# A float32r decoder block on one core: two products traded in each up pair, the down weights' low half by VectorE, and weight preparation in three steps

## The chip, the core and the metric

One core of one Trainium2 chip runs the whole program. The metric is device time in microseconds for one execution. A profiled execution also has a span, from its first instruction to its last, which is a little shorter than its time.

## The reference

One decoder block over 512 positions and 16 prepended meta tokens (528 in all), width 1024, in float32. The first half (attention, pooling, gates) is not touched. The second half is a gated MLP with a short convolution:

```python
h = h + (gate_a * y_a + gate_b * y_b) @ w_o[l]
hn = rmsnorm(h, norm2_g[l])
up = causal_dwconv(hn @ w_up[l], conv_w[l], conv_b[l])
a, bv = jnp.split(up, 2, axis=-1)
h = h + (jax.nn.silu(a) * bv) @ w_down[l]
...
return rmsnorm(h, final_norm_g)[:, N_META:]
```

`w_up` is 1024 x 5632 and `w_down` 2816 x 1024.

## The kernel before

Activations lie with channels on the 128 partitions and positions along the row. To keep float32 accuracy with float32r matmuls, each operand is split in a high half (the value rounded to float32r) and a low half (the value less its high half), and each product is three matmuls: high by high, high by low, low by high.

The MLP is a list `seq` of 38 jobs (lines 630 to 637). 22 are up jobs; job `up i` computes block `i` of `a` and block `i` of `bv` together, called an up pair here. 16 are down jobs, each two 128-row output blocks of `w_down` over one of four parts of the gated rows: parts 0 to 2 have six blocks of 128 rows (36 matmuls of 512 columns a job), part 3 has four (24). Two down jobs stand behind each of up 9, 10, 15 and 16; the other eight stand at the end, the last four of them (part 3) in a loop of their own (lines 856 to 889), where the final norm is worked in.

Up jobs 0 to 3 (`up_plain`, line 720) are plain products, while the four operand sets for the rest are made (`cross`, line 752). Up jobs 4 to 21 (`up_fast`, line 780) replace eight block products by seven, Strassen's way, each 4 x 3 = 12 matmuls of 258 columns into a PSUM bank (`seven`, line 771). Three products use weight blocks directly (`g`), four use sums of weight blocks (`sa`, `sb`). They run in this order: `x`, `q`, `v`, `x`, `y`, `x`, `q`. The second and third `x` add onto the first in the same bank, and the second `q` onto the first; between them ScalarE copies the running value out: `z11` (line 788), `z22` (790), `z12` (793), `z21` (797). So PE may not start the third `x` product before `z12` has been copied.

Four things make a job's weights:
- `fetch` (line 640): SP loads the raw tile, 1 MB for an up pair, 768 or 512 KB for a down job. There are three raw buffers (`raw`).
- `make_own` with `high_and_low` (lines 653 to 677): ScalarE writes the rounded negative of the raw weights to the low tile (`gl`, line 654), POOL issues DMAs that add the raw weights from memory onto it (line 656: three pieces of 256 KB for an up pair, two for a down job), and ScalarE copies the raw weights to the high tile (`gh`, line 657). There are two buffers of each, so those of job n + 2 are free when PE has ended job n.
- `make_sums` (line 682), for up jobs only: VectorE adds raw blocks in place (line 692, four adds), and `split` (line 248: a ScalarE copy at 249, a VectorE subtraction at 250) makes high and low halves of `sa` and `sb`.
- `prepare(n)` at the end of job n fetches for jobs n + 2 and n + 3 and calls `make_own(n + 2)`; in a fast up job those instructions are queued behind the `z21` copy. `weights(n)` at the start of job n calls `make_sums` for n and n + 1.

Each engine runs its queue in order. The framework (Tile) sets that order when the program is built: an instruction that it reckons to be ready sooner may be put ahead of one that the program lists earlier, and `tc.issue_after(ins)` forces what is traced in it, on the engine of `ins`, behind `ins`. It also makes the waits.

After up job i comes `conv(i - 3)` (line 808): the convolution taps, the gate and the split of the gated rows, on ScalarE and VectorE. After the last up job come the convolutions that are left.

Of the kernel before, what the change touches and what calls it, by code (L numbers as in the profile page):

```python
# [9 lines left out]
F32R = mybir.dt.float32r  # L10
BF16 = mybir.dt.bfloat16
I32 = mybir.dt.int32
AF = mybir.ActivationFunctionType
ALU = mybir.AluOpType

P = 128
# [20 lines left out]
PLAIN = 4  # L37
LAG = 3
CROSS = {(0, 1): 0, (1, 0): 1, (1, 1): 2, (2, 0): 3}
PARTS = ((0, 6), (6, 6), (12, 6), (18, 4))  # L40
# [28 lines left out]
def hybrid_block(ctx: ExitStack, tc: tile.TileContext, xt, g1d, wts, wup, wdown, wglr, wgk, vecs, out):  # L69
# [178 lines left out]
    def split(hi, lo, src):  # L248
        act.activation(hi, src, AF.Copy)
        dve.tensor_tensor(lo, src, f32(hi), ALU.subtract)  # L250
# [47 lines left out]
    for k in range(KT):  # L298
        for m in range(2):
            hi, lo = preps[m]  # L300
# [266 lines left out]
    for m in range(8):  # L567
        hi, lo = chunk(ORDER["grp"] + m // 4)
        acc = ps(f"pgrp{m}")
        g = m // 2  # L570
# [69 lines left out]
    def fetch(n):  # L640
        if n >= len(seq) or n in loaded:
            return
        job = seq[n]
        t = rawp.tile([P, 4, 512], F32, tag="raw", name=f"raw{n}")
        if job[0] == "up":
            sp.dma_start(t, wup[job[1]])
        else:
            nk = PARTS[job[1]][1]
            flat_t = t.rearrange("p a b -> p (a b)")
            sp.dma_start(flat_t[:, 0 : 2 * nk * P], wdown[4 * job[1] + job[2], :, 0 : 2 * nk * P])  # L650
        loaded[n] = t

    def high_and_low(hi, lo, src, dram, pieces):
        act.activation(lo, src, AF.Copy, scale=-1.0)  # L654
        for piece in pieces:
            pool.dma_start(lo[piece], dram[piece], accum_op=ALU.add)  # L656
        act.activation(hi, src, AF.Copy)  # L657

    def blocks(t):
        return t.rearrange("p a (k n) -> p a k n", n=P)  # L660

    def make_own(n):
        if n >= len(seq) or n in own:
            return
        fetch(n)
        job, raw = seq[n], loaded[n]
        hl = [gp.tile([P, 3, 512], F32R, tag=f"g{c}", name=f"g{c}{n}") for c in "hl"]
        if job[0] == "down":
            k = 2 * PARTS[job[1]][1] * P
            hi, lo, src = (t.rearrange("p a b -> p (a b)")[:, 0:k] for t in (*hl, raw))  # L670
            halves_of = [(slice(None), slice(c * k // 2, (c + 1) * k // 2)) for c in range(2)]
            high_and_low(hi, lo, src, wdown[4 * job[1] + job[2], :, 0:k], halves_of)
            own[n] = [t.rearrange("p (c k n) -> p c k n", c=2, n=P) for t in (hi, lo)]
            return
        order = (2, 0, 1) if job[1] >= PLAIN else (1, 2, 0)
        high_and_low(*hl, raw[:, 0:3], wup[job[1], :, 0:3], [(slice(None), b) for b in order])
        own[n] = [blocks(t) for t in hl]

    def two(name):
        return tuple(ssp.tile([P, 2, 4, P], F32R, tag=f"s{c}", name=f"s{c}_{name}") for c in "hl")  # L680
# [1 line left out]
    def make_sums(n):  # L682
        if n >= len(seq) or n in sums or seq[n][0] == "down":
            return
        raw = loaded[n]
        if seq[n][1] < PLAIN:
            x = two(f"{n}x")
            split(*(t[:, 0:1] for t in x), blocks(raw[:, 3:4]))
            sums[n] = (x,)
            return  # L690
        for dst, x in ((0, 3), (3, 2), (2, 0), (1, 2)):
            dve.tensor_tensor(raw[:, dst], raw[:, dst], raw[:, x], ALU.add)  # L692
        sums[n] = (two(f"{n}a"), two(f"{n}b"))
        split(*sums[n][0], blocks(raw[:, 0:3:2]))
        split(*sums[n][1], blocks(raw[:, 1:4:2]))

    def weights(n):
        make_sums(n)
        make_sums(n + 1)
        return (own[n], *sums.get(n, ()))  # L700

    def prepare(n, behind=None):
        fetch(n + 2)
        fetch(n + 3)
        if behind is None:
            make_own(n + 2)
        else:
            with tc.issue_after(behind.ins):
                make_own(n + 2)

    for n in range(2):
        make_own(n)

    def pairtile(name, dt=F32):
        return flat(name, unitp, dt)
# [3 lines left out]

    def up_plain(n, i):  # L720
        g, x = weights(n)
        z = pairtile(f"z{i}").rearrange("p (a b) -> p a b", a=2)
        for c in range(2):
            accs = [bank(f"pup{i}_{c}{h}") for h in range(2)]
            for k in range(KT):
                w = [
                    (x[e][:, 0, k // 2] if k % 2 else g[e][:, 0, k // 2]) if c
                    else g[e][:, 2 if k % 2 else 1, k // 2]
                    for e in range(2)
                ]  # L730
                for e, (p, q) in enumerate(((0, h2h), (0, h2l), (1, h2h))):
                    for acc, (a, b) in zip(accs, TAIL):
                        pe.matmul(  # L733
                            acc[:, 0 : b - a], w[p], q[k][:, a:b],
                            start=k == 0 and e == 0, stop=k == KT - 1 and e == 2,
                        )
            if i == 0 and c == 0:
                s2 = [bank(f"n2s{h}") for h in range(2)]
                for q, first_q in ((sh, True), (sl, False)):
                    for acc, (a, b) in zip(s2, TAIL):  # L740
                        pe.matmul(acc[:, 0 : b - a], ones, q[:, a:b], start=first_q, stop=not first_q)
                rsqrt_mean(rstd2, s2, TAIL, D, n2t)
            for src, cols in parts_of(accs, TAIL):
                dve.tensor_tensor(z[:, c, cols], src, rstd2[:, cols], ALU.mult)
            if (i, c) in CROSS:
                cross(CROSS[i, c])
        prepare(n)
        zs[i] = z
# [22 lines left out]
    def seven(acc, w, block, x, at, first=True):  # L771
        for k in range(4):
            for e, (a, b) in enumerate(((0, 0), (0, 1), (1, 0))):
                pe.matmul(  # L774
                    acc[:, 0:HN], w[a][:, block, k], x[k][b][:, at],
                    start=first and k == 0 and e == 0, stop=k == 3 and e == 2,
                    skip_group_check=not first,
                )

    def up_fast(n, i):  # L780
        g, sa, sb = weights(n)
        z = pairtile(f"z{i}").rearrange("p (a b) -> p a b", a=2)
        z11, z12 = (z[:, 0, a:b] for a, b in HALF)
        z21, z22 = (z[:, 1, a:b] for a, b in HALF)
        x, y, q, v_ = (bank(f"{c}{i}") for c in "xyqv")
        n_ = slice(0, HN)
        seven(x, g, 2, direct, 2)
        act.activation(z11, x[:, n_], AF.Copy)
        seven(q, sa, 0, crossed, 1)
        act.activation(z22, q[:, n_], AF.Copy)  # L790
        seven(v_, g, 0, crossed, 3)
        seven(x, sa, 1, crossed, 2, False)
        act.activation(z12, x[:, n_], AF.Copy)
        seven(y, g, 1, direct, 0)
        dve.tensor_tensor(z11, y[:, n_], z11, ALU.add)
        seven(x, sb, 1, crossed, 0, False)
        behind = act.activation(z21, x[:, n_], AF.Copy, scale=-1.0)
        dve.tensor_tensor(z22, z21, z22, ALU.subtract)
        dve.tensor_tensor(z21, v_[:, n_], z21, ALU.add)
        seven(q, sb, 0, direct, 1, False)  # L800
        dve.tensor_tensor(z12, q[:, n_], z12, ALU.add)
        prepare(n, behind)
        zs[i] = z

    gated = {}
# [28 lines left out]
    for n, job in enumerate(seq):  # L834
        if job[0] == "up":
            i = job[1]
            (up_plain if i < PLAIN else up_fast)(n, i)
            if i >= LAG:
                conv(i - LAG)
            if i == FF - 1:  # L840
                for k in range(FF - LAG, FF):
                    conv(k)
                table(LOG_EXP, silus[-1])
        elif job[1] < 3:
            (w,) = weights(n)
            for c in range(2):
                acc = bank(f"pd{n}_{c}")
                down(acc, w, c, job[1], (0, 512))
                h = h2[2 * job[2] + c][:, META:]
                dve.tensor_tensor(h, acc, h, ALU.add)  # L850
            prepare(n)
# [3 lines left out]
    base = len(seq) - 4  # L855
    for m in range(7):
        (w,) = weights(base + m // 2)
        if m % 2:
            prepare(base + m // 2)
        acc = bank(f"pe{m}")  # L860
        down(acc, w, m % 2, 3, (0, 512))
        h = h2[m][:, META:]
        dve.tensor_tensor(h, acc, h, ALU.add)
        if m == 0:
            act.activation(tot3, h, AF.Square)
        else:
            sq = pairtile(f"n3_sq{m}")[:, 0:512]
            act.activation(sq, h, AF.Square)
            (pool if m < 5 else dve).tensor_tensor(tot3, tot3, sq, ALU.add)
        act.activation(h, h, AF.Copy, scale=v1("gf", m))  # L870
# [94 lines left out]
```

## Time and profile before

| what | value |
|---|---|
| time, median of 3 runs | 854.01 us (851.27 to 854.12) |
| the profiled execution's own time | 854.07 us |
| its span | 852.4 us |
| mean granted TensorE clock | 0.994 of full |
| VectorE, ScalarE busy from 778 to 812 us | 17.74, 18.53 us of 34 |
| raw loads of up pairs | 22 of 1024 KB, median 8.0 us to landing |

Rows of the profile give the line of the kernel, the engine, the operation, the tile written and the tiles read (buffer numbers left out), the shape and a count. PE is the matmul engine, PEld its weight load, DVE is VectorE, ACT is ScalarE, POOL is GpSimd, SP the queue that issues plain loads. "Idle before, releaser" is the time in which an engine had nothing to run, and what ended it. In rows in order of time the first number is the start and the second the duration. Matmuls overlap, so the distance of two starts, not the duration, is what one costs. The MLP begins at about 476 us.

### The profile page before, as it was taken

The page shows a single profiled execution, that of the slowest core. Times are in us where ns is not written, and L with a number is a line of the kernel's source. Part 1 is how long each engine was busy: PE and PEld are TensorE (multiplying, and loading weights), DVE is VectorE, ACT ScalarE, POOL GpSimd, SP SyncE. Part 2 cuts the span into 40 slices and gives each one's busy share as a digit, 9 for nine tenths or more (in the row PEclk, how much of TensorE's full clock was granted, in tenths as well). Part 3 has the DMA queues.
Part 4 walks back from the last instruction along what each step waited for, and adds up shares of the span by engine and source line. Part 5 has one row for each costly group of instructions (what it writes and reads, how often), then busy time and mean ns, then how long its engine had stood idle before and what let it go on. Part 6 is the DMA issues. An engine that isn't in the chain of part 4 may idle for free.

```text
span 852.4 us, 15085 instructions
## 1 busy us (share of the span) xinstructions
PE 827.7 (97%) x6357; PEld 795.8 (93%) x6357; DVE 526.2 (62%) x817; ACT 440.4 (52%) x622; POOL 144.2 (17%) x149
## 2 busy tenths in 40 slices
PE   8999999999999999999999999999999999999993
PEld 6999999999999999999999999998899987999772
DVE  6677335379756433355555488995569844897425
ACT  7287134266234212353263357885568854777562
POOL 3000000001740000000022122221222222221241
PEclk9999999999999999999999999999999999999997
DMA  7423221122323322362275074867977777877763
GB/s 240 128 64 110 76 75 50 33 77 66 118 81 99 100 86 89 100 198 83 92 248 173 1 172 100 194 154 198 216 167 161 183 177 184 185 162 174 152 92 102
DMA packets 35780, 109.96 MB, mean 129 GB/s; under 512 B 4000, under 2 KB 6816, under 8 KB 32896
## 3 DMA queue, kind: packets, MB, share of 16 engines
q1 hardware_dynamic: 20368, 79.10, 27.8%
q0 software_dynamic: 14112, 28.84, 20.5%
q8 instruction: 50, 0.82, 0.4%
q10 hardware_dynamic: 1232, 1.05, 0.4%
q14 instruction: 18, 0.15, 0.0%
HBM read 106.88 MB, written 2.10 MB: 128 GB/s over the span
## 4 chain that ended last, share of the span: by engine, by line
PE 79%; DMA 7%; ACT 6%; DVE 5%; issue 2%; SPq 0%; DVEq 0%; POOL 0%; ACTq 0%
PE pd L829 9%; PE pu L150 5%; PE pv L150 5%; PE po L150 5%; PE pb L150 5%; PE pgb L150 5%; PE pga L150 5%; PE pr L150 5%; PE pa L150 5%; PE x L774 5%; DMA gl<-in_wdown_dram 5%; PE pup L733 4%; PE q L774 4%; PE pq L150 3%; DVE raw L692 2%
## 5 line engine op out<-in xcount | busy, mean ns | idle before, releaser
L133 ACT ACTIVATE whi<-wraw 128x1024 fp32r<-128x1024 f32 (+2 forms) x78 | 78.9, 1014 | 202.5 <-PE pa L150 36.4
L134 DVE TENSOR_TENSOR wlo<-wraw,whi 128x1024 fp32r<-128x1024 f32 (+2 forms) x78 | 94.8, 1218 | 13.0 <-ACT whi L133 7.2
L656 POOL DMA_DIRECT2D gl<-in_wup_dram x66 | 59.1, 1219 | 226.7 <-ACT gl L654 215.4
L829 PE MATMUL pd<-g,gh 128*128 128x512 f32 (+1 forms) x304 | 93.2, 388 | 0.0
L657 ACT ACTIVATE gh<-raw 128x1536 fp32r<-128x1536 f32 (+1 forms) x38 | 54.5, 1435 | 47.1 <-issue 26.1
L829 PEld LDWEIGHTS pd<-g,gh 128*128 128x128 f32 x304 | 56.5, 188 | 11.9
L829 PE MATMUL pd<-g,gl 128*128 128x512 f32 (+1 forms) x152 | 59.3, 390 | 3.2 <-DMA gl<-in_wdown_dram 3.2
L692 DVE TENSOR_TENSOR raw<-raw 128x512 f32<-128x512 f32 x72 | 49.5, 688 | 15.6 <-ACT gl L654 12.0
L654 ACT ACTIVATE gl<-raw 128x1536 fp32r<-128x1536 f32 (+1 forms) x38 | 54.4, 1431 | 0.8 <-DMA raw<-in_wup_dram 0.5
L535 POOL TENSOR_TENSOR pt<-u 128x1028 f32<-128x1028 f32 (+3 forms) x4 | 14.0, 3498 | 191.9 <-ACT whi L133 179.0
L656 POOL DMA_DIRECT2D gl<-in_wdown_dram x32 | 28.1, 1040 | 106.1 <-ACT gl L654 94.7
L850 DVE TENSOR_TENSOR h<-pd,h 128x512 f32<-128x512 f32 x24 | 16.5, 689 | 42.9 <-PE pd L829 42.8
L829 PEld LDWEIGHTS pd<-g,gl 128*128 128x128 f32 x152 | 28.6, 188 | 10.8 <-DMA gl<-in_wdown_dram 3.8
L815 DVE SCALAR_TENSOR_TENSOR cv<-z,vec,cv 128x512 f32<-128x512 f32 x44 | 32.7, 748 | 9.1 <-ACT cv L814 9.0
L814 ACT ACTIVATE cv<-z,vec 128x512 f32<-128x512 f32 x44 | 34.0, 812 | 0.0
L816 DVE SCALAR_TENSOR_TENSOR cv<-z,vec,cv 128x512 f32<-128x512 f32 x44 | 32.5, 747 | 0.2
L150 PE MATMUL pr<-xh,whi 128*128 128x258 f32 (+1 forms) x128 | 26.1, 285 | 0.0
L150 PE MATMUL pv<-xh,wlo 128*128 128x264 f32 x128 | 26.0, 285 | 0.0
L150 PE MATMUL pu<-xh,wlo 128*128 128x258 f32 (+3 forms) x128 | 25.9, 284 | 0.0
L150 PE MATMUL pv<-xl,whi 128*128 128x264 f32 x128 | 25.9, 284 | 0.0
L150 PE MATMUL pu<-xh,whi 128*128 128x258 f32 (+3 forms) x128 | 25.9, 284 | 0.0
L150 PE MATMUL pu<-xl,whi 128*128 128x258 f32 (+3 forms) x128 | 25.9, 284 | 0.0
(821 smaller groups left out, 2756.2 us busy)
## 6 DMA issues: line engine op xcount, KB each, us to landing
wraw<-in_wts_dram SPq DMA_DIRECT2D x72, 512.0 KB, 3.6
raw<-in_wup_dram SPq DMA_DIRECT2D x22, 1024.0 KB, 8.0
gl<-in_wup_dram POOLq DMA_DIRECT2D x66, 256.0 KB, 7.4
raw<-in_wdown_dram SPq DMA_DIRECT2D x12, 768.0 KB, 7.9
gl<-in_wdown_dram POOLq DMA_DIRECT2D x24, 384.0 KB, 8.1
h<-in_xt_dram SPq DMA_DIRECT2D x4, 514.0 KB, 6.0
raw<-in_wdown_dram SPq DMA_DIRECT2D x4, 512.0 KB, 4.8
gl<-in_wdown_dram POOLq DMA_DIRECT2D x8, 256.0 KB, 5.7
```

The lines of the kernel that those rows point to most:

```text
L133: act.activation(hi[:, a:b], t[:, a:b], AF.Copy)
L134: dve.tensor_tensor(lo[:, a:b], t[:, a:b], f32(hi[:, a:b]), ALU.subtract)
L150: pe.matmul(acc[:, s, : b - a], w, x[:, a:b], start=(i == 0 and w is wh and x is xh), stop=(i == n - 1 and last),)
L654: act.activation(lo, src, AF.Copy, scale=-1.0)
L656: pool.dma_start(lo[piece], dram[piece], accum_op=ALU.add)
L657: act.activation(hi, src, AF.Copy)
L692: dve.tensor_tensor(raw[:, dst], raw[:, dst], raw[:, x], ALU.add)
L733: pe.matmul(acc[:, 0 : b - a], w[p], q[k][:, a:b], start=k == 0 and e == 0, stop=k == KT - 1 and e == 2,)
L774: pe.matmul(acc[:, 0:HN], w[a][:, block, k], x[k][b][:, at], start=first and k == 0 and e == 0, stop=k == 3 and e == 2, skip_group_check=n ...
L814: act.activation(cv, z[:, c, META:], AF.Identity, scale=v1("cw2", m), bias=v1("cb", m))
L815: dve.scalar_tensor_tensor(cv, z[:, c, META - 1 : L - 1], v1("cw1", m), cv, ALU.mult, ALU.add)
L829: pe.matmul(acc, w[p][:, c, k], gated[k0 + k][q][:, a:b], start=k == 0 and e == 0, stop=k == nk - 1 and e == 2,)
```

## The change

In `up_fast` the order of the last two products is traded: `x`, `q`, `v`, `x`, `y`, `q`, `x`. The `z12` addition follows `q`, and `z21` is now copied from the last product.

`make_own` is split in two functions and a shared one. `direct_tiles(n)` takes the two tiles. `make_low(n)` makes the low tile of an up job as before (ScalarE negative, POOL DMAs) and does nothing for a down job. `make_high(n)` copies the high tile of an up job; for a down job it calls `split`, so that ScalarE makes the high tile and VectorE subtracts for the low one, with no DMA.

The calls move. `make_low(n + 2)` stays at the end of job n, behind the `z21` copy in fast up jobs. `make_high(n + 1)` and `make_sums(n + 1)` are called in job n: at its start in plain up jobs and down jobs, behind the `z11` copy in fast up jobs (the sums follow it in the program, without the forced order). Before the first job only `make_low(0)` and `make_low(1)` are called.

```diff
+    def make_low(n):
+        if n >= len(seq) or seq[n][0] == "down" or n in low_made:
             return
...
+        act.activation(lo, loaded[n][:, 0:3], AF.Copy, scale=-1.0)
+        for b in (2, 0, 1) if i >= PLAIN else (1, 2, 0):
+            pool.dma_start(lo[:, b], wup[i, :, b], accum_op=ALU.add)
+
+    def make_high(n):
...
+        _, (hi, lo), k = direct_tiles(n)
+        if k is None:
+            act.activation(hi, loaded[n][:, 0:3], AF.Copy)
+        else:
+            split(hi, lo, loaded[n].rearrange("p a b -> p (a b)")[:, 0:k])
...
     def weights(n):
+        make_low(n)
+        make_high(n)
         make_sums(n)
-        make_sums(n + 1)
-        return (own[n], *sums.get(n, ()))
-
-    def prepare(n, behind=None):
+        return (own[n][0], *sums.get(n, ()))
+
+    def behind(ins, made, n):
+        if ins is None:
+            return made(n)
+        with tc.issue_after(ins.ins):
+            made(n)
+
+    def prepare(n, ins=None):
         fetch(n + 2)
         fetch(n + 3)
...
+        behind(ins, make_low, n + 2)
...
         seven(x, g, 2, direct, 2)
-        act.activation(z11, x[:, n_], AF.Copy)
+        behind(act.activation(z11, x[:, n_], AF.Copy), make_high, n + 1)
+        make_sums(n + 1)
         seven(q, sa, 0, crossed, 1)
...
         dve.tensor_tensor(z11, y[:, n_], z11, ALU.add)
+        seven(q, sb, 0, direct, 1, False)
+        dve.tensor_tensor(z12, q[:, n_], z12, ALU.add)
         seven(x, sb, 1, crossed, 0, False)
-        behind = act.activation(z21, x[:, n_], AF.Copy, scale=-1.0)
+        turned = act.activation(z21, x[:, n_], AF.Copy, scale=-1.0)
         dve.tensor_tensor(z22, z21, z22, ALU.subtract)
         dve.tensor_tensor(z21, v_[:, n_], z21, ALU.add)
-        seven(q, sb, 0, direct, 1, False)
-        dve.tensor_tensor(z12, q[:, n_], z12, ALU.add)
-        prepare(n, behind)
+        prepare(n, turned)
...
         elif job[1] < 3:
             (w,) = weights(n)
+            make_high(n + 1)
+            make_sums(n + 1)
...
         (w,) = weights(base + m // 2)
+        make_high(base + m // 2 + 1)
```

More of the change, by code (lines that the diff above doesn't have):

```diff
@@ L651, in fetch @@
         loaded[n] = t
[L653 to L657, printed above, removed]
     def blocks(t):
         return t.rearrange("p a (k n) -> p a k n", n=P)
-    def make_own(n):
-        if n >= len(seq) or n in own:
-            return
[L665 to L673, printed above, removed]
-            return
-        order = (2, 0, 1) if job[1] >= PLAIN else (1, 2, 0)
-        high_and_low(*hl, raw[:, 0:3], wup[job[1], :, 0:3], [(slice(None), b) for b in order])
-        own[n] = [blocks(t) for t in hl]
@@ new lines, in hybrid_block, with direct_tiles @@
+    low_made, high_made = set(), set()
+    def direct_tiles(n):
+        if n not in own:
+            fetch(n)
+            job = seq[n]
+            hl = [gp.tile([P, 3, 512], F32R, tag=f"g{c}", name=f"g{c}{n}") for c in "hl"]
+            if job[0] == "down":
+                k = 2 * PARTS[job[1]][1] * P
+                hl = [t.rearrange("p a b -> p (a b)")[:, 0:k] for t in hl]
+                own[n] = [t.rearrange("p (c k n) -> p c k n", c=2, n=P) for t in hl], hl, k
+            else:
+                own[n] = [blocks(t) for t in hl], hl, None
+        return own[n]
@@ new lines, in make_low @@
+    def make_low(n):
+        if n >= len(seq) or seq[n][0] == "down" or n in low_made:
+            return
+        low_made.add(n)
+        _, (hi, lo), _ = direct_tiles(n)
+        i = seq[n][1]
+        act.activation(lo, loaded[n][:, 0:3], AF.Copy, scale=-1.0)
+        for b in (2, 0, 1) if i >= PLAIN else (1, 2, 0):
+            pool.dma_start(lo[:, b], wup[i, :, b], accum_op=ALU.add)
+    def make_high(n):
+        if n >= len(seq) or n in high_made:
+            return
+        high_made.add(n)
+        _, (hi, lo), k = direct_tiles(n)
+        if k is None:
+            act.activation(hi, loaded[n][:, 0:3], AF.Copy)
+        else:
+            split(hi, lo, loaded[n].rearrange("p a b -> p (a b)")[:, 0:k])
@@ L697, in weights @@
     def weights(n):
+        make_low(n)
+        make_high(n)
         make_sums(n)
-        make_sums(n + 1)
-        return (own[n], *sums.get(n, ()))
-    def prepare(n, behind=None):
+        return (own[n][0], *sums.get(n, ()))
[5 more added lines that the diff above has]
+    def prepare(n, ins=None):
         fetch(n + 2)
         fetch(n + 3)
[L705 to L712, printed above, removed]
+        behind(ins, make_low, n + 2)
+    make_low(0)
+    make_low(1)
     def pairtile(name, dt=F32):
@@ L845, in hybrid_block @@
             (w,) = weights(n)
+            make_high(n + 1)
+            make_sums(n + 1)
             for c in range(2):
```

## The prediction

> **What bounds the kernel now.** I read the page's engine table first, then the busy time by stage, the waits of PE, and last the rows of single instructions around each wait.
>
> ```profile
> PE 827.7 (97%) x6357; PEld 795.8 (93%) x6357; DVE 526.2 (62%) x817; ACT 440.4 (52%) x622; POOL 144.2 (17%) x149
> ```
>
> PE is busy nearly throughout, so its matmuls are the floor, and an edit that takes none away (this one takes none: the same seven products, the same down products) can only win back what PE idles. The edited code runs from about 476 us to the end. There PE waits for these (columns: who waited for whom, total us, times, longest):
>
> ```profile
> PE pd L829 <- DMA gl<-in_wdown_dram: 3.2, 4, 1.7
> PE x L774 <- ACT z L793: 1.2, 6, 0.2
> ```
> ```profile
> PE pe L829 <- DMA gl<-in_wdown_dram: 0.7, 2, 0.5
> PE pup L733 <- DMA gl<-in_wup_dram: 0.6, 1, 0.6
> ```
>
> The low half of a down weight arrives late six times (3.9 us), and the third `x` product of an up pair waits six times for the copy `z12` (1.2 us). VectorE looks far from full at 62%, but that is a mean over unlike stages (columns by stretch: length, then busy time and count of PE, PEld, DVE, ACT, POOL):
>
> ```profile
> 544.00:554.00 10.00, 10.00 (x86) 10.00 (x85) 10.00 (x18) 8.85 (x14) 2.64 (x3) 1.00 0.77 183
> 647.00:657.50 10.50, 10.29 (x87) 10.09 (x86) 10.11 (x17) 8.38 (x13) 2.64 (x3) 1.00 0.72 162
> ```
>
> Where up pairs follow one another, DVE has no gap in the first stretch and little in the second. VectorE work added to such a job would move the end; where it is added decides.
>
> **Part 1: the down weights' low half by VectorE.** An idle entry understates what a stall costs, because it counts from the modelled end of a matmul that others would have overlapped:
>
> ```profile
> 710.00 0.50 PE L829 MATMUL pd<-g,gl 128*128 128x512 f32 x1 [1.70 <-DMA gl<-in_wdown_dram]
> 710.33 0.61 PE L829 MATMUL pd<-g,gh 128*128 128x512 f32 x2
> 710.78 0.39 PE L829 MATMUL pd<-g,gl 128*128 128x512 f32 x1
> ```
>
> Two matmuls start in 710.78 - 710.33 = 0.45 us, 0.23 each, while one is shown as 0.39: a stall hides 0.16 more. The matmul behind the stalled one starts 0.33 later, not 0.23: 0.10 more. Six stalls therefore cost 3.9 + 6 x 0.26 = 5.5 us. Their cause is a chain as long as a job (rows of ACT, then of the chain that ended last):
>
> ```profile
> 601.74 1.49 ACT L657 ACTIVATE gh<-raw 128x1536 fp32r<-128x1536 f32 x1 [1.57 <-PE pd L829]
> 603.13 1.47 ACT L654 ACTIVATE gl<-raw 128x1536 fp32r<-128x1536 f32 x1
> ```
> ```profile
> 604.89 7.67 DMA gl<-in_wdown_dram
> 612.61 16.41 PE pd L829 x70
> ```
>
> A `g` buffer is free when the job two places earlier ends (601.7); two copies and 7.67 us of accumulating DMA later it is 612.56, and PE has been waiting. A down job lasts 16.41 / 2 = 8.2 us. The new chain has no DMA: copy `gh`, then one DVE subtraction. No row has that subtraction at 1536 columns; two rows of the same line give its slope:
>
> ```profile
> L657 ACT ACTIVATE gh<-raw 128x1536 fp32r<-128x1536 f32 x32 | 47.3, 1479 | 35.5 <-PE pd L829 16.8 <-issue 15.3 <-PE pup L733 3.4
> L250 DVE TENSOR_TENSOR g<-cv,g 128x512 fp32r<-128x512 f32 x22 | 15.2, 689 | 6.2 <-ACT g L249 6.2
> L250 DVE TENSOR_TENSOR xl<-t,xh 128x1032 fp32r<-128x1032 f32 x4 | 4.9, 1232 | 2.6 <-ACT xh L249 2.6
> L657 ACT ACTIVATE gh<-raw 128x1024 fp32r<-128x1024 f32 x4 | 4.2, 1060 | 11.6 <-issue 10.7 <-PE pe L829 0.9
> ```
>
> (1232 - 689) / 520 = 1.044 ns a column, so 1232 + 504 x 1.044 = 1758 ns for 1536 columns and about 1.22 us for 1024. The chain is 1.48 + 1.76 = 3.2 us within 8.2, and in the last four 1.06 + 1.22 = 2.3 us within twice the distance of these rows, 5.6:
>
> ```profile
> 815.29 0.69 DVE L863 TENSOR_TENSOR h<-pe,h 128x512 f32<-128x512 f32 x1 [2.09 <-PE pe L829]
> 818.07 0.69 DVE L863 TENSOR_TENSOR h<-pe,h 128x512 f32<-128x512 f32 x1 [2.08 <-PE pe L829]
> ```
>
> DVE gains 12 x 1.76 + 4 x 1.22 = 26 us of work. It lies in down jobs and in the up job ahead of a pair of them, and that up job makes no sums for its successor: it loses four adds and two splits and gains one split. So PE sees nothing of it: 0 us, and all 5.5 won. If the cover fails, the price is the rival A below. ACT loses 16 copies, POOL 32 DMA issues, the 16 DMA engines 11.3 MB; none sets the pace.
>
> **Part 2: the traded products.** Now `z12` has one product (`y`) of time before PE writes that bank again:
>
> ```profile
> 646.01 0.28 PE L774 MATMUL y<-dl,gh 128*128 128x258 f32 x1
> 646.13 0.28 PE L774 MATMUL y<-dh,gl 128*128 128x258 f32 x1
> 646.62 0.39 PE L774 MATMUL x<-xh,sh_16b 128*128 128x258 f32 x1 [0.20 <-ACT z L793]
> 646.84 0.28 PE L774 MATMUL x<-xl,sh_16b 128*128 128x258 f32 x1
> ```
>
> Here 0.49 passes in place of 0.12, then 0.22 in place of 0.12: 0.47 us, six times, 2.8 us. The copy is late because it stands behind a longer loop on ACT:
>
> ```profile
> 638.12 1.48 ACT L654 ACTIVATE gl<-raw 128x1536 fp32r<-128x1536 f32 x1
> ...
> 640.45 1.48 ACT L657 ACTIVATE gh<-raw 128x1536 fp32r<-128x1536 f32 x1
> ...
> 645.23 1.06 ACT L249 ACTIVATE sh_17a<-raw 128x1024 fp32r<-128x1024 f32 x1 [0.84 <-DVE raw L692]
> 646.20 0.36 ACT L793 ACTIVATE z<-x 128x258 f32<-128x258 f32 x1
> ```
>
> `z21` releases `gl`, then `gh`, then DVE's sums, then `sh_17a`, then `z12`, then PE, then the next `z21`. That closes each 10.5 us. With `q` between `y` and `x` the copy has 12 x 0.12 = 1.43 us more, against a lateness of 0.37: the loop opens and 2.8 us are won, if nothing else delays the copy (part 3). `q`'s own copy `z22` is four products old by then: 0.
>
> **Part 3: three separate steps.** `gh` of the next job is now queued behind `z11`, after `gl`, and the sums wait for it. The job in the rows above began five products, 7.2 us, ahead of 646.25 (where its third `x` would have begun without the stall), at 639.1. There `gh` ended at 641.9, 2.8 us in, and `z12` at 646.56, 7.5 us in. After the change ACT does `z21` (0.1 us in), `gl`, `z11` and `gh`; a wide copy takes 1.39 us there before the next starts (601.74 to 603.13), a narrow one like `z21` 0.28 (542.75 to 543.03, rows below), so `gh` ends 0.1 + 2 x (0.28 + 1.39) = 3.4 us in, 0.6 later. If `z12` stays behind `sh_a` it ends 8.1 us in, and PE wants it six products, 8.6 us in: 0.5 us to spare, 0 lost. In plain pairs and down jobs nothing orders `gh` behind `gl`; the rows at 601.74 show `gh` first although the program lists it second, so I leave the 0.6 us of the plain pair where it is (bounds: 0 to 0.85 won, at the cost per stall above).
>
> What moves for the worse is `gl` of an up pair behind `z21`, now the last product's copy, 1.43 us later. POOL's DMAs and all that waits in POOL's queue behind them move too (rows of ACT, POOL; then DMA issues: count, KB, us to landing):
>
> ```profile
> 542.75 0.39 ACT L797 ACTIVATE z<-x 128x258 f32<-128x258 f32 x1 [0.49 <-PE x L774]
> ```
> ```profile
> 544.81 2.64 POOL L656 DMA_DIRECT2D gl<-in_wup_dram  x3 [7.41 <-ACT gl L654]
> ```
> ```profile
> gl<-in_wup_dram POOLq DMA_DIRECT2D x1, 256.0 KB, 4.4
> ```
> ```profile
> raw<-in_wup_dram SPq DMA_DIRECT2D x1, 1024.0 KB, 5.9
> gl<-in_wup_dram POOLq DMA_DIRECT2D x1, 256.0 KB, 7.7
> ```
> ```profile
> gl<-in_wdown_dram POOLq DMA_DIRECT2D x1, 384.0 KB, 9.5
> ```
> ```profile
> DMA to landing us min/median/max: 3.9/7.4/13.6
> ```
>
> The first piece leaves 2.06 us behind the start of `z21`, which will be about 0.1 us into the next job: issue at +2.1. The job after needs it at 7 x 1.43 + 0.24 = +10.3. It may take 8.2 us. It took 4.4 where the 1 MB raw load came later, 7.7 where that load went out with it (the two rows are one answer, for 526.2 to 526.55). So 0.5 us is left in the worst like case: 0 us. [...]
>
> **Sum.** The profiled execution took 854.07 us (span 852.4), 0.06 over the median 854.01. 854.07 - 5.5 - 2.8 = 845.8 us.
>
> **Rivals.**
> A: the late VectorE split. After the last up pair the convolutions 19 to 21 come ahead of the new split in the program, and DVE takes its queue in order:
>
> ```profile
> 781.89 0.75 DVE L815 SCALAR_TENSOR_TENSOR cv<-z,vec,cv 128x512 f32<-128x512 f32 x1 [1.82 <-ACT cv L814]
> ...
> 786.70 0.68 DVE L850 TENSOR_TENSOR h<-pd,h 128x512 f32<-128x512 f32 x1
> ```
>
> At 781.9 ten convolution steps of at most 0.75 us and six of 0.69 are still to come: 11.6 us, to 793.5, and the split behind all of it ends at 795.3. PE wants it when this down job is over, by the second row at about 786.6. That would be 8.7 us, 854.5, and half of it, 850.2, if the split slips in midway; I take 852, between the two. For it: program order. Against: the gap of 1.82 us, in which a split fits, and the down sum of the second row, later still in the program, that stands between such steps.
>
> B, the slower side: the first low piece lands late. Place: the ten hand-overs where an up pair's `gl` waits behind `z21` of a pair two before. It decides from 8.2 us to landing on. If it takes the 9.5 us seen for a larger piece beside raw loads, each loses 9.5 - 8.2 = 1.3 us, 13 in all: 859. For it: raw loads are released by the same sums and may now run first. Against: no 256 KB first piece took over 7.7.
>
> C: the swap doesn't do what it says. The 0.5 us to spare is used up, by the rounding of both sums ahead of `z12` or a slower DVE, and the wait is back one product later at the old price of 2.8: 848.6.
>
> **How the numbers follow.** A difference within 0.5% (4.3 us) is about what a measurement here can't tell from none. Forecast 0.51 (faster), C 0.15 (faster), A 0.18 (same), B 0.16, of which 0.14 slower and 0.02, with small lateness, same. Faster 0.66, same 0.20, slower 0.14. The range begins at 843.0 (the forecast, less 0.85 for the plain pair, and 2 us for runs that scatter as 851.27 to 854.12 do). It ends at 853.5, past most of A, and leaves out most of B.
>
> **What would show it.** Right: no row of PE waiting for `gl` from the down weights; 16 subtractions of about 1.76 and 1.22 us on DVE; no wait of `x` for `z12`; up pairs 10.05 us apart in the late runs too. Wrong: PE waiting for a DVE `gl` near 786 (A), for a DMA `gl` from the up weights at the start of an up job (B), or for ACT's `z12` (C).

## The result

| | before | after |
|---|---|---|
| time, median of 4 runs each, same chip | 854.07 us (851.27 to 854.50) | 843.54 us (842.50 to 844.33) |
| ratio, 95% interval | | 0.9883 [0.9859, 0.9907] |
| profiled execution's own time, span | 854.07, 852.4 us | 842.50, 840.2 us |
| mean granted TensorE clock | 0.994 | 0.996 |
| start of the first up matmul to start of the last norm matmuls | 362.56 us | 353.46 us |
| from there to the end of the span (spans known to 0.1 us) | 13.28 us | 11.14 us |

The kernel is 10.5 us, 1.2%, faster; 8.3 us was forecast (845.8 us, range 843.0 to 853.5). Sign and range held. The two profiled executions differ by 11.57 us: 9.10 in the MLP, about 2.1 behind its last matmuls, 0.96 in a start-up that no edited line touches, less about 0.6 outside the span. The 2.1 had no term in the forecast, and the experiments show that one of the forecast's two terms belongs to another edit.

The engine table of the page after, then every wait of PE that the list of waits names from 470 us on (who waited for whom, total us, times, longest):

```profile
PE 824.1 (98%) x6357; PEld 796.1 (95%) x6357; DVE 548.8 (65%) x833; ACT 420.7 (50%) x606; POOL 117.2 (14%) x117
```
```profile
PE n3s L900 <- ACT sq L899: 0.9, 1, 0.9
PE pup L750 <- DVE h L603: 0.8, 1, 0.8
PE n3s L896 <- DVE sq L890: 0.7, 1, 0.7
```

Neither the down weights nor `z12` are in the list. What it still names is the entry into the MLP and the final norm. The stretches that answer those of before (length, then busy time and count of PE, PEld, DVE, ACT, POOL):

```profile
543.00:553.00 10.00, 10.00 (x84) 9.87 (x84) 9.62 (x17) 8.26 (x13) 2.65 (x3) 1.00 0.84 179
647.00:657.00 10.00, 10.00 (x86) 10.00 (x85) 9.90 (x17) 7.67 (x12) 2.65 (x3) 1.00 0.81 175
```

Ten microseconds now hold a late up pair that took 10.5. VectorE has no more to do for it than it had (9.90 us in 10.00 against 10.11 in 10.50), but it is even fuller. Its new work in the list of groups, and three of these subtractions in order of time:

```profile
L250 DVE TENSOR_TENSOR gl<-raw,gh 128x1536 fp32r<-128x1536 f32 (+1 forms) x16 | 26.0, 1622 | 6.6 <-ACT gh L249 6.4
```
```profile
764.90 1.76 DVE L250 TENSOR_TENSOR gl<-raw,gh 128x1536 fp32r<-128x1536 f32 x1
770.49 1.75 DVE L250 TENSOR_TENSOR gl<-raw,gh 128x1536 fp32r<-128x1536 f32 x1
779.91 1.76 DVE L250 TENSOR_TENSOR gl<-raw,gh 128x1536 fp32r<-128x1536 f32 x1 [0.60 <-ACT gh L249]
```

The first ends at 766.66, ahead of its job, whose first matmul starts at 770.10. And the drain of GpSimd that closes the kernel (durations in ns: shortest, median, longest), before and after:

```profile
L960 POOLq DRAIN  x3: 40/93/7737, 843.8 to 852.1; - x3
```
```profile
L981 POOLq DRAIN  x3: 40/93/5123, 833.8 to 840.0; - x3
```

It is 2.61 us shorter, and the end of the span follows it.

### The profile page after: what moved, and what is told of

Read it like the earlier page. It is cut to its first block, busy times and chain, and to the rows that moved or that the text cites. A ratio compares the mean times of both kernels' runs of the same rounds, so it can differ in the third digit from the quotient of the medians.

```text
span 840.2 us, 15052 instructions
## 1 busy us (share of the span) xinstructions
PE 824.1 (98%) x6357; PEld 796.1 (95%) x6357; DVE 548.8 (65%) x833; ACT 420.7 (50%) x606; POOL 117.2 (14%) x117
## 4 chain that ended last, share of the span: by engine, by line
PE 94%; DVE 2%; DMA 2%; ACT 1%; issue 0%; SPq 0%; DVEq 0%; POOL 0%; ACTq 0%
PE pd L847 12%; PE x L791 9%; PE q L791 6%; PE pu L150 6%; PE pv L150 6%; PE po L150 5%; PE pb L150 5%; PE pr L150 5%; PE pgb L150 5%; PE pga L150 5%; PE pa L150 5%; PE pup L750 4%; PE y L791 3%; PE v L791 3%; PE pq L150 3%; PE pe L847 2%
## 5 line engine op out<-in xcount | busy, mean ns | idle before, releaser
L687 ACT ACTIVATE gh<-raw 128x1536 fp32r<-128x1536 f32 x22 | 32.7, 1484 | 27.6 <-PE pd L847 24.3
L677 ACT ACTIVATE gl<-raw 128x1536 fp32r<-128x1536 f32 x22 | 32.5, 1477 | 2.8 <-PE pd L847 2.2
L250 DVE TENSOR_TENSOR gl<-raw,gh 128x1536 fp32r<-128x1536 f32 (+1 forms) x16 | 26.0, 1622 | 6.6 <-ACT gh L249 6.4
L249 ACT ACTIVATE gh<-raw 128x1536 fp32r<-128x1536 f32 (+1 forms) x16 | 22.0, 1376 | 11.7 <-PE pd L847 9.2
```

The costliest lines, as they stand in the source:

```text
L677: act.activation(lo, loaded[n][:, 0:3], AF.Copy, scale=-1.0)
L687: act.activation(hi, loaded[n][:, 0:3], AF.Copy)
```

## The experiments

The first seven kernels are the change taken apart: the trade of the two products (T), the low part of the down weights by VectorE (V), the separate steps (S). Each ratio is to runs of the kernel before in the same series (medians 854.07, 854.85, 854.93 and 855.52 us in the four series). The last column is the length of the MLP in the profiled execution, counted as in the table above.

| kernel | median us | ratio to before, 95% | MLP us |
|---|---|---|---|
| before | 854.07 | 1 | 362.56 |
| T | 861.65 | 1.0084 [1.0061, 1.0107] | 369.42 |
| V | 845.70 | 0.9885 [0.9868, 0.9902] | 356.61 |
| S | 852.06 | 0.9967 [0.9952, 0.9982] | 360.52 |
| T + V | 845.33 | 0.9892 [0.9876, 0.9908] | 356.68 |
| T + S | 858.36 | 1.0046 [1.0030, 1.0062] | 368.35 |
| V + S | 843.87 | 0.9861 [0.9844, 0.9878] | 354.06 |
| V + S, again | 843.83 | 0.9859 [0.9836, 0.9881] | 354.25 |
| T + V + S, the change | 843.54 | 0.9883 [0.9859, 0.9907] | 353.46 |
| the change, again | 844.02 | 0.9873 [0.9859, 0.9888] | 355.48 |

**V alone.** The edit to the kernel before, in the branch for down jobs:

```diff
-            high_and_low(hi, lo, src, wdown[4 * job[1] + job[2], :, 0:k], halves_of)
+            split(hi, lo, src)
```

> The kernel before with only the low half of the down weights made by a VectorE subtraction in make_own; product order and preparation order as before. Theory S: the six waits for the DMA low half go (5.5 us), the six for z12 stay (2.8 us): 848.5 us by PE's waits; and if the 2.1 us by which the program's tail behind the last matmul is shorter after the change (11.1 for 13.3 us) belongs to the 32 DMAs that POOL no longer issues, 846.4 us and a POOL drain near 5 us in place of 7.7. Rival L: without the separate steps the split stands behind z21 two jobs ahead, where VectorE is full, and pushes z12 or the sums: more z12 waits, 849 to 851 us.

845.7 us: theory S holds. Its waits of PE for the MLP:

```profile
PE x L774 <- ACT z L793: 1.3, 6, 0.2
PE pup L733 <- DMA gl<-in_wup_dram: 0.5, 1, 0.5
```

All waits for the down weights are gone, and the MLP is 5.95 us shorter, where 5.5 was forecast. Its drain took 5122 ns, so the 2.1 us at the end are V's too. The `z12` waits stay.

**T alone.**

```diff
+        seven(q, sb, 0, direct, 1, False)
+        dve.tensor_tensor(z12, q[:, n_], z12, ALU.add)
         seven(x, sb, 1, crossed, 0, False)
         behind = act.activation(z21, x[:, n_], AF.Copy, scale=-1.0)
         dve.tensor_tensor(z22, z21, z22, ALU.subtract)
         dve.tensor_tensor(z21, v_[:, n_], z21, ALU.add)
-        seven(q, sb, 0, direct, 1, False)
-        dve.tensor_tensor(z12, q[:, n_], z12, ALU.add)
```

> The kernel before with only the last two products traded; everything else, the DMA low halves of the down weights included, as before. Theory S (each edit wins its own waits, whatever else is there): the six waits of x for z12 go, 2.8 us, 851.2 us; the six waits for the down weights' low half stay at 5.5 us. Rival L (the edits lean on each other): z21 comes one product, 1.43 us, later, and with it the low half of the down weights that are made behind it, so the wait in the second down job behind up 9 (0.81 us before) grows to about 2.2; 852.6 us. In both the program's tail from the last matmul on stays at 13.3 us.

861.65 us, slower by 0.8%: both theories missed. No `z12` wait is left, yet late up pairs stand 10.33 to 10.37 us apart, a little less than the 10.52 to 10.54 of before but more than 10.06, and the down weights come later than before:

```profile
PE pd L829 <- DMA gl<-in_wdown_dram: 9.3, 6, 2.5
...
PE pe L829 <- DMA gl<-in_wdown_dram: 0.8, 2, 0.4
```

The down weights make most of the loss: these waits are 10.1 us in place of 3.9, and the MLP is 6.86 us longer. Why the up pairs are still slow stands in ScalarE's rows and in PE's rows of the same pair, which began at 651.79:

```profile
652.89 0.37 ACT L799 ACTIVATE z<-x 128x258 f32<-128x258 f32 x1
653.15 1.48 ACT L654 ACTIVATE gl<-raw 128x1536 fp32r<-128x1536 f32 x1
654.53 1.47 ACT L657 ACTIVATE gh<-raw 128x1536 fp32r<-128x1536 f32 x1
655.90 0.62 ACT L249 ACTIVATE g<-cv 128x512 fp32r<-128x512 f32 x1
656.42 0.37 ACT L788 ACTIVATE z<-x 128x258 f32<-128x258 f32 x1
```
```profile
656.59 0.28 PE L774 MATMUL y<-dl,gh 128*128 128x258 f32 x1
656.84 0.39 PE L774 MATMUL x<-xh,sh_17a 128*128 128x258 f32 x1
```

The rows of L799, L654, L657 and L788 are `z21`, `gl`, `gh` and `z11`. The turned quarter `z21` is now copied from the last product, and all that is queued behind it on ScalarE starts later by that product. `z11` ends at 656.79, and PE's second `x`, which adds onto the bank that `z11` is read from, starts at 656.84. The order built even puts five matmuls of `y` ahead of that `x`, and 0.13 us is still lost, with 0.11 at the next matmul. The wait has moved from `z12` to `z11`. The same happens in early up pairs, which ran 10.06 us apart before and now stand 10.38 to 10.47 apart.

**S alone, and V + S.** Of the change, only the split of the preparation into separate steps; V + S has VectorE's low parts as well, so it is the change without the trade.

```diff
-        act.activation(z11, x[:, n_], AF.Copy)
+        behind(act.activation(z11, x[:, n_], AF.Copy), make_high, n + 1)
+        make_sums(n + 1)
```

> The changed kernel with both other edits undone: the product order of before, the down weights' low half again by POOL's accumulating DMAs, but low half, high half and sums as three separate steps. Theory S: no wait goes or comes, 854 us. Rival L: the high half behind z11 starts the sums 0.6 us later, and without the trade z12 has only one product of time, so each of the ten or so late closings of the loop costs 0.6 us more than the 0.47 of before: 857 to 860 us, with z12 waits of about 0.8 us in the trace.

> The changed kernel with the product order of before. Theory S: the changed kernel plus the z12 waits, 843.5 + 2.8 = 846.3 us. Rival L: the z12 waits come back larger than they were (0.6 us each on top, about ten of them), 850 to 853 us, so the trade is worth more beside the steps than alone.

852.06 and 843.87 us: both theories missed both, on the slow side of what came. The steps alone win, 0.33%, and V + S is as fast as the whole change. ScalarE's rows tell why. First V, then V + S in its second profile (L793 and L811 are `z12`):

```profile
642.77 1.06 ACT L249 ACTIVATE sh_17a<-raw 128x1024 fp32r<-128x1024 f32 x1 [0.84 <-DVE raw L692]
643.74 0.37 ACT L793 ACTIVATE z<-x 128x258 f32<-128x258 f32 x1
```
```profile
642.00 0.39 ACT L811 ACTIVATE z<-x 128x258 f32<-128x258 f32 x1 [0.33 <-PE x L791]
642.80 1.07 ACT L249 ACTIVATE sh_17a<-raw 128x1024 fp32r<-128x1024 f32 x1 [0.41 <-DVE raw L704]
...
652.37 1.06 ACT L249 ACTIVATE sh_18a<-raw 128x1024 fp32r<-128x1024 f32 x1 [0.58 <-DVE raw L704]
653.33 0.36 ACT L811 ACTIVATE z<-x 128x258 f32<-128x258 f32 x1
```

In V, ScalarE stood idle for 0.84 us until VectorE's sums let `sh_17a` start, with `z12` behind it in the queue, whose product ended at 642.51, inside that gap. With the steps the sums come later in the program, and `z12` stands ahead of `sh_17a` and runs in such a gap. Only in two pairs, the one of the last two rows among them, does it still stand behind the next pair's first sums, and in a third behind a convolution step and a split of gated rows. PE waits in these three alone:

```profile
PE x L791 <- ACT z L811: 0.8, 3, 0.3
```

The MLP is 356.61 - 354.06 = 2.55 us shorter for it (2.36 in the second run). That is most of the 2.8 us that the prediction gave to the trade.

**T with V, T with S, and the change again.** These are combinations of the edits shown above.

> The trade and VectorE's low parts, without the separate steps (both copies of an up pair's weights stay together behind the turned quarter). Theory Q, the order of ScalarE's queue decides: with the trade alone the copies gl and gh stand ahead of z11 on ScalarE, and the second x product waits for z11 in every late up pair; taking the down weights' DMAs away doesn't change that. Up jobs 10.3 to 10.4 us apart; against the run with VectorE's low parts alone (845.7 us) it loses 13 small waits of 0.25 to 0.35 us and wins six of 0.47: 845.5 to 847.5 us. Rival W, the trade alone was slow only because it pushed the down weights' DMAs later: with those gone the up jobs run at 10.07 us and the time is that of the whole change, 843 to 844 us.

845.33 us, a hair under theory Q's range, with late up pairs 10.34 to 10.37 us apart: Q holds, W falls. Beside V (356.61 against 356.68 us) the trade alone is worth nothing: what `z12` no longer costs, `z11` does, early pairs included, and two waits for the low part of a fast up pair that V doesn't have:

```profile
PE x L774 <- DMA gl<-in_wup_dram: 0.7, 2, 0.4
```

> The trade and the separate steps, with the low part of the down weights still by DMA. Theory Q: the up jobs run 10.07 us apart as in the whole change, since gh now stands behind z11; but z21 and so the low copy start about 1 us later than without the trade, and every down job waits longer for its DMA: the separate steps alone had 4.4 us of these waits, here 7 to 10 us; the end of the kernel is 2.1 us longer than in the whole change. Sum: 843.5 + 2.1 + 7 to 10 = 852.5 to 855.5 us. Rival W, the trade costs the down weights nothing once the steps are separate: 843.5 + 2.1 + 4.4 = 850 us.

858.36 us, above both. Up pairs mostly ran 10.06 us apart, as Q said. The waits for the down weights' DMAs, issued later, are within the 7 to 10 us that Q allowed (8.8 here, and 0.4 in the last loop):

```profile
PE pd L854 <- DMA gl<-in_wdown_dram: 8.8, 5, 4.2
```

But the longest of these waits cost more than its length. PE's rows at it, and two stretches (length, busy times, then the granted clock in the third column from the end):

```profile
806.35 0.77 PE L854 MATMUL pd<-g,gl 128*128 128x512 f32 x1 [4.16 <-DMA gl<-in_wdown_dram]
806.92 1.05 PE L854 MATMUL pd<-g,gh 128*128 128x512 f32 x2
807.77 0.63 PE L854 MATMUL pd<-g,gl 128*128 128x512 f32 x1
```
```profile
795.00:802.00 7.00, 7.00 (x32) 5.49 (x30) 2.50 (x5) 3.97 (x5) 1.75 (x2) 1.00 0.33 78
806.00:813.00 7.00, 6.65 (x18) 5.25 (x19) 0.05 (x1) 0.00 (x0) 0.00 (x0) 0.57 0.68 153
```

Behind a wait of 4.16 us two matmuls take 0.85 us, not 0.46, and the granted clock is 0.57. From 806.92 to 812.04 us thirteen matmuls came 0.2 us later each, about 2.7 us in all: with it Q's sum is 843.5 + 2.1 + 9.2 + 2.7 = 857.5 us.

> The whole change once more, beside the others on the same chip. Both theories: a ratio of 0.986 to 0.990 to the kernel before.

844.02 us, ratio 0.9873. This profiled execution showed what the first had only in traces of 0.1 to 0.2 us:

```profile
PE x L791 <- DMA gl<-in_wup_dram: 1.0, 2, 0.6
...
PE pup L750 <- DMA gl<-in_wup_dram: 0.5, 1, 0.5
```
```profile
566.45 1.75 POOL L679 DMA_DIRECT2D gl<-in_wup_dram  x2 [7.41 <-ACT gl L677]
```
```profile
573.69 0.28 PE L791 MATMUL x<-dl,gh 128*128 128x258 f32 x1
574.57 0.39 PE L791 MATMUL x<-dh,gl 128*128 128x258 f32 x1 [0.60 <-DMA gl<-in_wup_dram]
```

The pieces left 3.1 us into a job that began at 563.32; the first was wanted at 573.69 + 0.12 = 573.81, 7.4 us later, and took 8.1. This is the prediction's rival B, in small, and for the reason it named: a raw load now goes out first.

```profile
565.81 0.33 SPq L650 DMA_DIRECT2D raw<-in_wdown_dram  x1
```

**The turned quarter ahead of the second sums.** In the change, ScalarE takes `sh_b` (the high part of the next pair's second sums) ahead of `z21` and `gl`. Here `sh_b` is put behind `z21`, and is taken behind `gl`:

```diff
-        make_sums(n + 1)
+        make_sums(n + 1, True)
...
         prepare(n, turned)
+        behind(turned, split_b, n + 1)
```

`make_sums(n, True)` leaves out its last `split`, and `split_b` does it.

> The whole change, with the copy that turns z21 and the low copy gl put ahead of the high part of the next pair's second sums (sh_b) on ScalarE. Theory B, the first piece of the next pair's low weights is what the trade puts at risk, because the turned quarter is now the last product: here GpSimd issues the pieces 1 us earlier, 1.6 to 2.1 us into the next job in place of 2.6 to 3.1, and the waits for gl of an up pair (0.38 and 0.60 us with small ones beside them in the second run of the whole change) go. Up jobs 10.05 to 10.07 us apart throughout, gaps on TensorE about 1 us less, 842 to 843.5 us, ratio 0.985 to 0.987. Rival C, the pieces land when the other transfers let them, so an earlier issue only means a longer flight: the waits stay, 844 us.

841.82 us (841.29 to 842.29), ratio 0.9835 [0.9812, 0.9858]: theory B holds, C falls. V + S, on the same chip in the same series, took 843.83 us (843.23 to 844.18). The change itself ran in other series (842.50 to 844.33 in its eight runs); no run of any other kernel here was as fast as the slowest of these five. ScalarE, GpSimd, PE and the raw load around the same hand-over as above:

```profile
562.53 0.39 ACT L826 ACTIVATE z<-x 128x258 f32<-128x258 f32 x1
562.82 1.48 ACT L677 ACTIVATE gl<-raw 128x1536 fp32r<-128x1536 f32 x1
564.20 1.05 ACT L249 ACTIVATE sh_8b<-raw 128x1024 fp32r<-128x1024 f32 x1
```
```profile
564.59 2.65 POOL L679 DMA_DIRECT2D gl<-in_wup_dram  x3 [7.41 <-ACT gl L677]
```
```profile
572.51 0.28 PE L800 MATMUL x<-dl,gh 128*128 128x258 f32 x1
572.64 0.28 PE L800 MATMUL x<-dh,gl 128*128 128x258 f32 x1
```
```profile
566.53 0.33 SPq L650 DMA_DIRECT2D raw<-in_wdown_dram  x1
```

The job began at 562.33, so the pieces left 2.3 us in and had 8.05 us; PE did not wait. The first piece needed only 4.29 us, since it left 1.94 us ahead of the raw load: the subtraction behind `sh_b`, which releases that load, is later too. So the edit doesn't only issue the pieces 0.9 us earlier, it shortens the flight of the first one, the opposite of rival C. Between the entry into the MLP and the final norm no gap over 0.08 us is left between PE's matmuls; the MLP takes 352.41 us. The trade is worth about 2 us after all (354.25 - 352.41 = 1.84 in the trace) once its own price is taken away. V + S has `z21` and `gl` ahead of `sh_b` on ScalarE already (655.27, 655.55 and 656.93 us in its first profile), so it is the right kernel to compare with.

> VectorE's low parts and the separate steps without the trade, once more, beside the version above. Theory B: no waits for gl of an up pair, a few waits for z12 (three of 0.3 us before), 843.5 to 844.2 us, ratio 0.986 to 0.988, no more than 0.3% from the whole change either way. Rival V, the trade is worth its own 2.8 us: 846 us.

843.83 us: the 846 us of rival V fall. This is the run "V + S, again" of the table.

**The late split, made on purpose.** In the change, the split of the first weights of down part 2 is queued on VectorE behind the product of convolution 19:

```diff
-        behind(act.activation(z11, x[:, n_], AF.Copy), make_high, n + 1)
+        first = act.activation(z11, x[:, n_], AF.Copy)
+        if i < FF - 1:
+            behind(first, make_high, n + 1)
...
-                    conv(k)
+                    product = conv(k)
+                    if k == FF - LAG:
+                        behind(product, make_high, n + 1)
```

> The whole change, but the split of the first weights of down part 2 is queued on VectorE behind the products of convolutions 18 and 19: the late split of the rival with VectorE, made on purpose, to learn its price. In the whole change this split ended at 766.6 us and its job began at 770.3; here it should end at about 778. Theory P, the price is the wait alone: TensorE waits 6 to 8 us once, span 846.5 to 850 us. Rival K, a wait of that length also costs the clock: in the run with the trade and the steps, the 20 matmuls behind a wait of 4.16 us came 0.43 us apart in place of 0.23: 3 to 4 us more, span 850 to 854 us.

One run, 850.29 us, span 847.9. The split, the matmul that waited for it, and the stretch around it, granted clock 0.76:

```profile
775.70 1.75 DVE L250 TENSOR_TENSOR gl<-raw,gh 128x1536 fp32r<-128x1536 f32 x1
```
```profile
777.51 0.79 PE L850 MATMUL pd<-g,gl 128*128 128x512 f32 x1 [5.27 <-DVE gl L250]
778.10 1.05 PE L850 MATMUL pd<-g,gh 128*128 128x512 f32 x2
778.95 0.63 PE L850 MATMUL pd<-g,gl 128*128 128x512 f32 x1
```
```profile
770.00:780.00 10.00, 4.73 (x18) 3.54 (x17) 9.16 (x15) 4.98 (x8) 0.00 (x0) 0.76 0.13 40
```

The wait is 5.27 us, a little below P's 6 to 8 (and behind the wait of 4.16 us, from which K takes its amount, 13 matmuls were slow, not 20); the gaps between PE's matmuls at this place add up to 7.6 us, of which 2.1 come from the slow matmuls behind the wait. The span lies in P's interval, but only with K's effect in it: the mechanism of both is there, K's amount for it was too large. Rival A had named the split of the second of these down jobs, wanted a job later; this is the price of a late split at the first.

**Fewer and more DMAs on GpSimd.** In the first kernel plain up pairs 1 to 3 get their low part by VectorE too, nine DMAs fewer:

```diff
-        if k is None:
+        if k is None and seq[n][1] in (1, 2, 3):
+            split(hi, lo, loaded[n][:, 0:3])
+        elif k is None:
```

In the second GpSimd issues 32 small DMAs more:

```diff
+    pad = pairtile("pad")[:, 0:256].rearrange("p (j e) -> p j e", e=8)
+    for j in range(32):
+        pool.dma_start(pad[0:P, j], wdown[0, 0:P, 8 * j : 8 * j + 8])
```

> The whole change, and the low part of the weights of plain up pairs 1 to 3 by VectorE too, so that GpSimd issues nine DMAs fewer. Theory D, the drain of GpSimd at the end of the kernel grows with the number of DMAs that it has issued (32 fewer took it from 7.74 to 5.12 us, 82 ns each): the drain takes 4.4 us, the last wait of a plain pair (0.35 us near 500 us) goes, and the span falls from 840.2 to about 839.1 us. Rival E, the drain has a long and a short form, according to what is in flight in the last stage: it stays at 5.1 us, span about 839.9 us. VectorE takes three operations of 1.76 us more in a stage with idle time, which by both costs nothing.

> The whole change with 32 more DMAs issued by GpSimd, of 128 rows of 32 bytes each, into a tile that nothing reads, behind the last low piece of the up pairs. Theory D, the drain at the end goes by the number of DMAs that GpSimd has issued: 98 as before the change, drain 7.74 us, span 2.6 us longer than without them (842.8 to 844.6 us). Rival F, it goes by what these DMAs move or add up: it stays at 5.12 us, span 840.2 to 842 us. The run with nine DMAs fewer spoke against D (6.55 us), so a third value here would leave the cause open.

843.93 us (ratio 0.9874 [0.9857, 0.9892]), as the change; and 845.85 us, one run. The drains, of the nine fewer and of the 32 more:

```profile
L983 POOLq DRAIN  x3: 40/102/6552, 835.0 to 842.1; - x3
```
```profile
L984 POOLq DRAIN  x3: 46/102/7730, 835.5 to 843.8; - x3
```

Both theories fall for the first kernel: with fewer DMAs the drain got longer, and the time is that of the change. The second bears D out: small plain copies in place of 384 and 256 KB additions bring the drain of before back, with 10528 packets on that queue where there were 14112. So in these runs the drain goes with how many DMAs GpSimd has issued, not with their size, but not in proportion: 57 gave 6.55 us, 66 gave 5.12 to 5.13 in all eight profiles with that number, 98 gave 7.73 to 7.74 in five. Why is open.

## Why the prediction was right, and where it was wrong

- **Part 1, 5.5 us by VectorE's low half: right.** Alone it shortened the MLP by 5.95 us. The price of the subtraction (1.76 us, 26 us in all) and its cover held; PE never waited for it.
- **What Part 1 left out.** It listed 32 POOL DMA issues as setting no pace. They do at the end of the kernel: the drain there was 2.6 us longer with them, of which 2.1 us show in the time.
- **Part 2, 2.8 us by the trade: the amount about right, the cause wrong.** The step that failed is "the loop opens and 2.8 us are won, if nothing else delays the copy". The separate steps open that loop without the trade (2.4 to 2.55 us). And the trade delays copies itself: `z21` stands one product later, and so does all that ScalarE queues behind it. Without the steps that is `z11` and in two places `gl`, and nothing is won (T + V); with them it is `gl`, and the gain is lost again at the hand-overs, in amounts that change from run to run (MLP 353.46 and 355.48 us, against 354.06 and 354.25 without the trade).
- **Part 3, 0 us: wrong.** It reckoned with "if `z12` stays behind `sh_a`", a condition that I didn't examine: the edit moves the sums in the program, and `z12` went ahead of `sh_17a`. Part 3 took the change in ScalarE's queue for a delay of 0.6 us and looked only for what `gh` would lose.
- **Issue of `gl` at +2.1 us: wrong by about 1 us.** It left 3.1 us into most jobs whose `gl` follows a `z21`, 3.8 into one, because `sh_b` stands ahead of `z21`. `sh_b` waits for the last product too: its buffer holds the sums which that product reads. So 7.2 to 7.4 us were left in most where 8.2 were forecast. The raw load went out ahead, and the first piece took 6.1 to 7.3 us in the first profile and up to 8.1 in the second, against 4.3 to 4.7 at these places before. Putting `sh_b` behind `gl` gave 2.3 and 8.05 us, nearly the forecast's numbers, and flights of 4.2 to 4.8 us.
- **The plain pair, left at 0 won, 0 to 0.85 allowed:** the gap before it was 0.24 and 0.61 us in the two runs of the change, 0.75 before: within the bounds.
- **Rival A did not come.** A fast up job reads its `g` weights last in `y`, two products before its end, so the high copy of the second down job's split was free to start before the job ended (767.28 in the change, released by `y`; the job ended at 770.10), and the order built puts the subtraction between convolution steps, at 770.49. Its price was named as 852 - 845.8 = 6.2 us; a late split one job earlier, made on purpose, cost 7.6.
- **Rival B came in part.** The place and the mechanism are those named, the raw load that runs first included. The price was not 13 us but about 1 and 3 us in the two profiles (353.46 and 355.48 against 352.41, of which 0.4 and 0.7 at a plain pair): in the second profile lateness was 0.4 and 0.6 us at two hand-overs and 0.1 to 0.2 at others, not 1.3 at ten. The argument against it, that no first piece took over 7.7 us, overlooked one before the MLP: issued at 444.06, it took 8.64. **Rival C did not come.**
- **The sum.** 5.5 held, 2.8 was won by another edit, 2.1 at the end was missing. The median came out 2.3 us under the forecast, about that missing term, and 0.5 us inside the range. That the sum came so near is partly luck: the steps happened to win about what had been put down to the trade. The signs named for a right forecast (no wait for down weights or `z12`, late up pairs near 10.05 us apart) showed, but they couldn't tell the trade from the steps; only the kernels with one edit left out could.

## What to carry to other kernels

When a step that feeds an in-order queue is moved, list what stands behind it in that queue with the time at which each is wanted, in the old order and the new. Here one product of delay, 1.43 us, took back the whole gain of the trade, at `z11` or at `gl`, until the copy behind which the transfer is queued was put first. Parts of a change that touch one queue aren't worth the sum of their separate gains: T lost 7 us alone and was worth about 2 us in the best version. And an instruction removed from an engine that sets no pace may still be on the path where the kernel closes, as 32 DMA issues of GpSimd were here, by 2.1 us.

## What the hardware did that I had not expected

- **Two long waits also cost clock.** Behind waits of 4.16 and 5.27 us, matmuls of 512 columns started 0.43 us apart in place of 0.23, until 5.7 and 4.4 us after the wait; the 7 us around the first had a granted clock of 0.57. Behind the 1.70 us wait of the kernel before, the next matmul came 0.33 us later and those after it 0.23 us apart, at a granted clock of 1.00 from 708 to 712 us. T alone, with six waits of up to 2.5 us, had a mean granted clock of 0.995 over its span, against 0.994 before and 0.990 and 0.991 in the two runs with the long waits. Why, and from which length of wait on, these runs don't show.
- **The closing drain of GpSimd** took 6.6, 5.1 or 7.7 us in the runs where it had issued 57, 66 or 98 DMAs.
- **Which of two transfers left first went with how long each took.** At the ten places of rival B, in the kernel before, the first low piece of an up pair leaves about 2 us ahead of a raw load (768 KB or 1 MB); it lands after 4.3 to 4.7 us and the load after 7.4 to 9.1. In the change the raw load leaves first, by 0.2 to 1.3 us; there it takes 4.4 to 5.8 us and the piece 6.1 to 7.3. With `z21` put first the old order is back, and with it 4.2 to 4.8 and 7.5 to 8.7 us. The raw loads' median fell from 8.0 us before to 5.8 in the change, but the 32 DMAs fewer don't explain that alone: it is 7.3 with the same 66 DMAs in the version with `z21` first, and 6.7 with all 98 in T alone. The rows of the change and of the version with `z21` first:

```profile
raw<-in_wup_dram SPq DMA_DIRECT2D x22, 1024.0 KB, 5.8
```
```profile
raw<-in_wup_dram SPq DMA_DIRECT2D x22, 1024.0 KB, 7.3
```
